# The first x load of a batched matmul issued in two parts, rows 0 to 111 and rows 112 to 127

## The chip, the cores and the metric

The kernel runs on one core of a Trainium2 chip. The metric is the device time of one execution in microseconds (us), taken as the median of several runs. One further execution was recorded by the hardware profiler, and it is the one whose profile is read here.

## The reference

```
b1, b2, m, k, n = 8, 16, 256, 512, 384
x:      (8, 16, 256, 512) float32
weight: (8, 16, 512, 384) float32
out = np.matmul(x, weight).astype(np.float32)     # 128 separate products
```

There are 128 products of a 256x512 matrix with a 512x384 matrix. The inputs are 167.77 MB and the output is 50.33 MB, so that every byte is read or written once.

## The kernel before

**Groups.** The 128 products are worked off in NG = 32 groups of G = 4. A group needs one x load of 2048 KB (`load_x`, L121), weights of 3072 KB (`load_w`, L138), and one store of 1536 KB (`store`, L160). An x load fills one of two buffers `x_sb`, each of 128 partitions (called rows here) with R = 8 rows of x, 16 KB, side by side in each. The first four and the last two groups are "short": their weights come as two loads of 1536 KB, each with a semaphore of its own (`h_in`), the others as one (`w_in`).

**Engines.** VectorE (DVE) turns x into bf16 (`cast_x`, L194, four instructions a group) and casts most of the weights (`cast_w`, L207, and `cast_short`, L223). TensorE (PE) transposes x against an identity (L247) and multiplies (L265; L283 in the last group). ScalarE (ACT) copies the transposed x out of PSUM (L234), casts the rest of the weights (L207) and copies the results out (L300). GpSimd (POOL) makes the identity, and it stores one whole group (SHARED = 26) itself, in three pieces of 5, 120 and 3 rows (`store_rest`, L174).

**The order of the transfers.** SyncE (SP) issues all the other transfers, in an order that is written out by hand in `on_sync`: for each of the first four groups the x load and then the weights, then in a hardware loop x load, store and weights for each group, and at the end the last loads and the last five stores. An issue waits on its engine's own queue: an x load from the third on waits until the cast of the group two before is done (L114), the weights until the casts of the group two before are done (L132, L133). What SP has issued lies in one DMA queue (q1), which 16 DMA engines work off. At its end SP waits for the stores of the three groups before the last (`o_end`, L331), counts a spare semaphore up in a loop of four and PAD = 12 more times (L332 to L335), and waits for the last store (`o_fin`, L336).

**Around the change.** `load_x(e, 0, NG, 0)` is SP's first transfer (L317). `cast_x` waits for it before its first instruction (L190): the semaphore `x_in[0]` must have reached 16, which is what one transfer adds when it has landed. `next_x(0, NG, -1)` (L356) is the first thing that DVE does, and PE's first transposes (L371) and ACT's first copies (L405) follow it.

Of the kernel before, what the change touches and what calls it, by code (L numbers as in the profile page):

```python
# [12 lines left out]
def kernel(  # L13
# [47 lines left out]

    SHARED = NG - 2 - LAG

    ctx.enter_context(tc.tile_critical(sync_engine=mybir.EngineType.Pool, no_gpsimd_drain=True))  # L64

    def sbuf(name, shape, dtype, n):
# [9 lines left out]
    def sems(name, n):  # L76
        return [tc.alloc_semaphore(f"{name}{s}") for s in range(n)]
# [24 lines left out]
    h_in = sems("h_in", G)  # L102
    o_end = sems("o_end", 1)[0]
    rest_out = sems("rest_out", 1)[0]
    o_fin, spare = sems("o_fin", 1)[0], sems("spare", 1)[0]


# [3 lines left out]
    def load_x(e, t, U, s):  # L111
        n = t * U + s
        if not isinstance(n, int) or n >= XS:
            e.wait_ge(x_cast, n * T + (1 - XS) * T)  # L114
        rows = x_rows[bass.ds(n * (G * M), G * M)]
        if is_full(n):
            src = rows.rearrange("(i p r) k -> p i r k", i=G, p=P)
            dst = x_sb[s % XS][:].rearrange("p (i r) k -> p i r k", i=G)
        else:
            src, dst = rows.rearrange("(p r) k -> p r k", r=R), x_sb[s % XS][:]  # L120
        e.dma_start(dst, src).then_inc(x_in[s % XS], 16)  # L121

    def is_short(n):
        return isinstance(n, int) and (n < LAG or n >= NG - 2)

    def is_full(n):
        return isinstance(n, int) and n == NG - 1
# [59 lines left out]
    def cast_x(e, t, U, s, q):  # L187
        n = t * U + s
        if q == 0:
            e.wait_ge(x_in[s % XS], (t * (U // XS) + s // XS) * 16 + 16)  # L190
        e.wait_ge(t_made, n * T + (q + 1 - T + BIAS))  # L191
        rows = slice(2 * q, 2 * q + 2)
        S = SH if is_short(n) else SL
        e.tensor_copy(  # L194
            out=x_bf[s % BS][:, rows].rearrange("p r (s q c) -> p r s q c", s=S, c=KO),
            in_=x_sb[s % XS][:, rows].rearrange("p r (q s c) -> p r s q c", s=S, c=KO),
        ).then_inc(x_cast, 1)
# [116 lines left out]
    def on_sync(e):  # L314
        U = 2
        for n in range(LAG):
            load_x(e, 0, NG, n)  # L317
            load_w(e, 0, NG, n)
        rounds = (NG - 2 - LAG) // U
        with e.Fori(0, rounds) as t:  # L320
            for s in range(U):
                load_x(e, t, U, LAG + s)
                store(e, t, U, s)
                load_w(e, t, U, LAG + s)

        for n in range(LAG + rounds * U, NG):
            load_x(e, 0, NG, n)
            load_w(e, 0, NG, n)
        for n in range(NG - 1 - LAG, NG):
            store(e, 0, NG, n)  # L330
        e.wait_ge(o_end, 16 * (OS - 1))  # L331
        with e.Fori(0, 4):  # L332
            e.sem_inc(spare, 1)
        for _ in range(PAD):
            e.sem_inc(spare, 1)  # L335
        e.wait_ge(o_fin, 16)  # L336

    def on_vector(e):
        U = 2

        def next_x(t, U, s):
            for q in range(T):
                cast_x(e, t, U, s + 1, q)

        def step(t, U, s):
            n = t * U + s
            if is_short(n):
                cast_short(e, n)
            else:
                cast_w(e, t, U, s, range(XV))  # L350
            if not isinstance(n, int) or n < NG - 1:
                next_x(t, U, s)
            if not is_short(n):
                cast_w(e, t, U, s, range(XV, CV), False)

        next_x(0, NG, -1)  # L356
        for n in range(LAG):
            step(0, NG, n)
        rounds = (NG - 3 - LAG) // U
        with e.Fori(0, rounds) as t:  # L360
            for s in range(U):
                step(t, U, LAG + s)
        for n in range(LAG + rounds * U, NG):
            step(0, NG, n)
# [88 lines left out]
```

## Time and profile before

| what | us |
|---|---|
| median of 3 runs | 515.75 (515.63 to 515.79) |
| the profiled execution's own time | 516.01 |
| its span, first to last instruction | 514.2 |
| outside the span | 1.81 |
| DVE busy | 397.6 (77%) |
| ACT busy | 409.5 (80%) |
| PE busy | 316.8 (62%) |
| bytes moved | 218.18 MB, 424 GB/s over the span |

Busy times are sums over an engine's instructions. "DMA share" in a table of windows is the mean busy share of the core's 16 DMA engines in that stretch, as the profile sums it from packets; it can exceed 1.00 by a per cent where packets overlap. "KB" in the lists of transfers is 1024 bytes. "SPq" stands for what SP's queue issues, and "us to landing" is from the issue until the transfer's semaphore has its full count.

### The profile page before, as it was taken

How to read it: one execution, taken by the hardware profiler on the slowest of the kernel's cores; microseconds unless marked ns; L12 is line 12 of the kernel's file. 1: busy time of each engine (PE TensorE's matmuls, PEld its weight loads, DVE VectorE, ACT ScalarE, POOL GpSimd, SP SyncE). 2: the span in 40 equal slices, each digit the busy share in tenths (PEclk: the TensorE clock that was granted, in tenths of full speed). 3: DMA queues.
4: the chain of work that ended last, by engine and by line, in shares of the span. 5: the costliest groups of instructions: out<-in, count | busy, mean ns of one | idle time of the engine just before them, and what ended most of it. 6: DMA issues, size and time to landing. Idle time of an engine off the chain costs nothing.

```text
span 514.2 us, 11664 instructions
## 1 busy us (share of the span) xinstructions
PE 316.8 (62%) x4512; PEld 222.5 (43%) x4512; DVE 397.6 (77%) x462; ACT 409.5 (80%) x387; POOL 3.7 (1%) x9
## 2 busy tenths in 40 slices
PE   2277837556675575866568656567545676474782
PEld 2255525434454343544435534345434354353551
DVE  2788757798777887778977779777798777887980
ACT  1365576997898989789978989987998798989752
POOL 0000000000000000000000000000000000010000
PEclk9687785877787778668776868886878787778887
DMA  8999999999999999999999999999999999999997
GB/s 334 429 427 422 438 423 427 436 430 435 420 427 433 433 436 429 425 429 433 440 427 428 427 435 429 438 426 426 431 437 435 425 426 429 435 435 420 422 426 308
DMA packets 15686, 218.18 MB, mean 424 GB/s; under 512 B 1728, under 2 KB 1728, under 8 KB 3008
## 3 DMA queue, kind: packets, MB, share of 16 engines
q1 hardware_dynamic: 15312, 216.54, 98.8%
q0 software_dynamic: 368, 1.57, 0.7%
q8 instruction: 3, 0.05, 0.0%
q14 instruction: 3, 0.02, 0.0%
HBM read 167.77 MB, written 50.33 MB: 424 GB/s over the span
## 4 chain that ended last, share of the span: by engine, by line
DMA 55%; DVE 31%; issue 9%; PE 1%; DVEq 1%; SPq 1%; ACT 0%; POOLq 0%
DMA w_sb<-in_weight_dram 55%; DVE w_bf L207 20%; DVE w_bf L223 5%; DVE x_bf L194 5%; PE po L283 1%; SPq L138 0%; DVEq L360 0%; SPq L121 0%; DVEq L64 0%; DVEq L203 0%; ACT out_sb L300 0%; SPq L133 0%; DVEq L191 0%; DVEq L217 0%; SPq L448 0%
## 5 line engine op out<-in xcount | busy, mean ns | idle before, releaser
L207 DVE CAST w_bf<-w_sb 32x1536 bf16<-32x1536 f32 x286 | 271.9, 951 | 81.9 <-DMA w_sb<-in_weight_dram 70.7
L265 PE MATMUL po<-w_bf,x_t 128*32 128x384 bf16 x3968 | 197.1, 358 | 34.1 <-DVE w_bf L207 29.5
L247 PE MATMUL pt<-identity,x_bf 128*128 128x128 f32 x512 | 114.7, 414 | 153.5 <-DVE x_bf L194 153.5
L207 ACT CAST w_bf<-w_sb 32x1536 bf16<-32x1536 f32 x130 | 190.9, 1468 | 5.5 <-DMA w_sb<-in_weight_dram 2.3
L247 PEld LDWEIGHTS pt<-identity,x_bf 128*128 128x128 f32 x512 | 103.4, 224 | 165.4 <-issue 165.1
L265 PEld LDWEIGHTS po<-w_bf,x_t 128*32 128x32 bf16 x3968 | 116.1, 105 | 113.8 <-issue 53.0
L300 ACT COPY out_sb<-po 128x768 f32 (+1 forms) x128 | 102.5, 801 | 58.8 <-PE po L265 54.7
L234 ACT COPY x_t<-pt 128x1024 bf16<-128x1024 bf16 x128 | 123.6, 1020 | 21.2 <-PE pt L247 20.6
L194 DVE CAST x_bf<-x_sb 128x1024 bf16<-128x1024 f32 x128 | 79.9, 688 | 12.3 <-DMA x_sb<-in_x_dram 11.5
L223 DVE CAST w_bf<-w_sb 64x1536 bf16<-64x1536 f32 x48 | 45.8, 955 | 7.4 <-DMA w_sb<-in_weight_dram 6.0
L234 ACT ACT_TABLE_LOAD x1 | 1.3, 1283 | 10.6 <-PE pt L247 10.6
L174 POOL DMA_DIRECT2D out_dram<-out_sb x3 | 3.1, 1020 | 458.9 <-DMA out_dram<-out_sb 458.9
L283 PE MATMUL po<-w_bf,x_t 128*128 128x384 bf16 x32 | 5.4, 326 | 0.4 <-DVE w_bf L223 0.4
L283 PEld LDWEIGHTS po<-w_bf,x_t 128*128 128x128 bf16 x32 | 3.1, 98 | 2.7 <-issue 0.7
masks.py:199 POOL TENSOR_SCALAR_AFFINE_SELECT identity<-identity 128x128 f32<-128x128 f32 x1 | 0.3, 283 | 0.2 <-POOL identity L306 0.2
L306 POOL MEMSET identity<- 128x128 f32 x1 | 0.2, 204 | 0.5 <-POOLq L64 0.5
L437 POOL MEMSET const-bfloat16-1.0<- 128x1 bf16 x1 | 0.1, 96 | 0.0
L437 POOL MEMSET const-uint8-127<- 128x1 uint8 x1 | 0.1, 96 | 0.0
L437 POOL MEMSET const-float32-0.0<- 128x1 f32 x1 | 0.1, 93 | 0.3 <-issue 0.3
L437 POOL MEMSET const-float32-1.0<- 128x1 f32 x1 | 0.1, 93 | 0.0
## 6 DMA issues: line engine op xcount, KB each, us to landing
w_sb<-in_weight_dram SPq DMA_DIRECT2D x26, 3072.0 KB, 18.1
x_sb<-in_x_dram SPq DMA_DIRECT2D x32, 2048.0 KB, 22.3
out_dram<-out_sb SPq DMA_DIRECT2D x31, 1536.0 KB, 25.0
w_sb<-in_weight_dram SPq DMA_DIRECT2D x12, 1536.0 KB, 16.7
out_dram<-out_sb POOLq DMA_DIRECT2D x1, 1440.0 KB, 16.8
out_dram<-out_sb POOLq DMA_DIRECT2D x1, 60.0 KB, 7.1
out_dram<-out_sb POOLq DMA_DIRECT2D x1, 36.0 KB, 17.6
```

The source lines that it names most:

```text
L174: e.dma_start(out=dram[p : p + k], in_=out_sb[p : p + k, a : a + R], max_dma_last_dim=R // 2 * N * 4,).then_inc(rest_out, 16)
L194: e.tensor_copy(out=x_bf[s % BS][:, rows].rearrange("p r (s q c) -> p r s q c", s=S, c=KO), in_=x_sb[s % XS][:, rows].rearrange("p r (q s ...
L207: copy(out=w_bf[(s * G + i) % WBS][h * C : (h + 1) * C], in_=w_sb[s % WS][i * C : (i + 1) * C, h * KO : (h + 1) * KO, :],).then_inc(w_vcas ...
L223: e.tensor_copy(out=w_bf[(n * G + d * SH + a) % WBS][h * p : (h + 1) * p], in_=w_sb[n % WS][a * p : (a + 1) * p, r : r + KO, :],).then_inc ...
L234: e.copy(out=x_t[s % TS][:, 2 * q : 2 * q + 2], in_=pt[(s * T + q) % PT][:].bitcast(bf16),).then_inc(t_copied, 1)
L247: ins = e.transpose(pt[(s * T + q) % PT][:, rr, h, :], words[:, 2 * q + rr, h :: KO // 2], identity[:],)
L265: ins = e.matmul(po[(s * T + q) % PO][mine, rr, :N], x_t[s % TS][:, 2 * q + rr, ko // 2, mine, ko % 2], w_bf[(s * G + i) % WBS][:, ko, :], ...
L283: ins = e.matmul(po[(s * T + q) % PO][:, rr, :N], x_t[s % TS][:, 2 * q + rr, ko // 2, :, ko % 2], w_bf[(s * G + q) % WBS][:, ko, :], start ...
L300: e.copy(out=out_sb[:, bass.ds(slot(t, U, s) * R + 2 * q, 2), :], in_=po[(s * T + q) % PO][:, :, :N],).then_inc(o_copied, 1)
L306: e.memset(identity[:], 0.0).then_inc(id_done, 1)
L437: nc = _bacc.Bacc("TRN2", target_bir_lowering=False, num_devices=1)
```

## The change

The first x load, that of group 0, is issued as two transfers. The first has rows 0 to 111 of the buffer (112 x 16 KB = 1792 KB) and counts on a new semaphore `x_rest`; the second has rows 112 to 127 (16 x 16 KB = 256 KB) and counts on `x_in[0]`, as the whole load did. DVE's first cast waits for both. The other 31 x loads and every other instruction stay as they were.

```diff
@@ constants
+    FIRST = 112
@@ semaphores
+    x_rest = sems("x_rest", 1)[0]
@@ load_x
             src, dst = rows.rearrange("(p r) k -> p r k", r=R), x_sb[s % XS][:]
+        if isinstance(n, int) and n == 0:
+            e.dma_start(dst[:FIRST], src[:FIRST]).then_inc(x_rest, 16)
+            dst, src = dst[FIRST:], src[FIRST:]
         e.dma_start(dst, src).then_inc(x_in[s % XS], 16)
@@ cast_x
         if q == 0:
             e.wait_ge(x_in[s % XS], (t * (U // XS) + s // XS) * 16 + 16)
+            if isinstance(n, int) and n == 0:
+                e.wait_ge(x_rest, 16)
         e.wait_ge(t_made, n * T + (q + 1 - T + BIAS))
```

Built, SP's program has one transfer more (112x4096 and 16x4096 elements where 128x4096 stood), and DVE's has no row more: the first cast lists the semaphore x_rest beside the two for which it waited already. PE, ACT and POOL issue the same rows as before.

## The prediction

> **What bounds the kernel now.** I began with the page: its span, the DMA row of the 40 slices, and the chain that ended last.
>
> ```profile
> span 514.2 us, 11664 instructions
> ...
> DMA  8999999999999999999999999999999999999997
> ...
> DMA 55%; DVE 31%; issue 9%; PE 1%; DVEq 1%; SPq 1%; ACT 0%; POOLq 0%
> ```
>
> The DMA engines are nine tenths busy or more in every slice but the first and the last. The chain names DMA for 55%, and DVE for 31%, but DVE's steps on it are those that allow a later load to be issued, and the question is whether the DMA engines ever ran dry while they waited for that. The table of windows answers it.
>
> ```profile
> core 0: us, PE busy (x) PEld busy (x) DVE busy (x) ACT busy (x) POOL busy (x), PEclk, DMA share, GB/s
> 0.00:1.90 1.90, 0.00 (x0) 0.00 (x0) 0.00 (x0) 0.00 (x0) 0.69 (x6) 1.00 0.00 0
> 1.90:4.00 2.10, 0.00 (x0) 0.00 (x0) 0.00 (x0) 0.00 (x0) 0.00 (x0) 1.00 0.96 242
> 4.00:8.00 4.00, 0.00 (x0) 0.00 (x0) 0.00 (x0) 0.00 (x0) 0.00 (x0) 1.00 1.00 428
> 8.00:28.00 20.00, 8.48 (x72) 7.63 (x76) 14.66 (x19) 7.94 (x9) 0.00 (x0) 0.74 1.01 428
> 28.00:508.00 480.00, 308.34 (x4448) 214.90 (x4436) 382.94 (x444) 401.61 (x379) 3.05 (x3) 0.78 1.01 429
> 508.00:510.00 2.00, 0.00 (x0) 0.00 (x0) 0.00 (x0) 0.00 (x0) 0.00 (x0) 0.50 1.00 399
> 510.00:511.00 1.00, 0.00 (x0) 0.00 (x0) 0.00 (x0) 0.00 (x0) 0.00 (x0) 0.50 0.75 298
> 511.00:512.00 1.00, 0.00 (x0) 0.00 (x0) 0.00 (x0) 0.00 (x0) 0.00 (x0) 0.50 0.27 108
> 512.00:513.00 1.00, 0.00 (x0) 0.00 (x0) 0.00 (x0) 0.00 (x0) 0.00 (x0) 0.50 0.09 33
> 513.00:514.20 1.20, 0.00 (x0) 0.00 (x0) 0.00 (x0) 0.00 (x0) 0.00 (x0) 0.50 0.00 0
> ```
>
> The last two columns carry the argument. From about 1.9 us to 510 us the share is full and the rate stands at 428 to 429 GB/s: all 16 engines always have something queued. The kernel is one unbroken DMA stream, with 1.9 us before it and a ragged end. Between 510 and 513 us the share falls over 0.75, 0.27 and 0.09: some engines are done at 510, the last only after 512. So time that a DMA engine loses anywhere, the first load included, is not caught up; it reaches the end if that engine is among the late ones. Time that SP, DVE, ACT or PE lose costs nothing while the queue stays filled.
>
> **The issue itself.** The timeline of SP's queue shows the start.
>
> ```profile
> 0.90 0.39 SPq L121 DMA_DIRECT2D x_sb<-in_x_dram  x1
> 1.35 0.89 SPq L138 DMA_DIRECT2D w_sb<-in_weight_dram  x2
> 2.28 0.64 SPq L121 DMA_DIRECT2D x_sb<-in_x_dram  x1
> 2.97 0.99 SPq L138 DMA_DIRECT2D w_sb<-in_weight_dram  x2
> ...
> 11.18 0.33 SPq L121 DMA_DIRECT2D x_sb<-in_x_dram  x1
> 21.16 0.81 SPq L138 DMA_DIRECT2D w_sb<-in_weight_dram  x2
> ```
>
> One issue takes 0.39 to 0.64 us here. The change adds one, so five issues (two weight loads, the second x load, two more weight loads) come about 0.45 us later. Cover: the first part alone is 112 x 16 KB = 1,835,008 bytes, which at 428 GB/s is 4.29 us of stream from 1.9 us on, and the second part is issued by about 1.8 us, the first weights by about 2.2 us. Without cover it would be 0.45 us; with it, I take 0. The start of the stream should not move: it hangs on the first issue, which stays first. From the trace alone a shorter first issue could start it 0.05 us sooner (an eighth of 0.39).
>
> **The extra wait on DVE.** It comes with the first cast; behind it on DVE stand the whole casting program, behind that PE's first transposes, and SP's third x load.
>
> ```profile
> PE pt L247 <- DVE x_bf L194: 22.7, 3, 10.1
> ...
> DVE x_bf L194 <- DMA x_sb<-in_x_dram: 10.3, 3, 8.7
> ...
> 8.65 2.50 DVE L194 CAST x_bf<-x_sb 128x1024 bf16<-128x1024 f32 x4 [8.65 <-DMA x_sb<-in_x_dram]
> ...
> L121 SPq DMA_DIRECT2D x_sb<-in_x_dram x4: 328/358/642, 0.9 to 24.7; - x4
> ...
> DMA to landing us min/median/max: 7.7/20.9/23.2
> ```
>
> DVE waits 8.7 us for that load already, the first PE and ACT work follows it, and both parts must land as the one load had to: a wait for two costs nothing of its own. If the second part lands L us later, DVE, PE and ACT start L later, and SP's issues at 11.18 and 21.16 us come L later. What covers them is the queue: when the first load lands (0.90 + 7.7 = 8.6 us) there remain four weight loads of 1536 KB and one x load of 2048 KB, 8.39 MB, 19.6 us at 428 GB/s, until about 28 us; with the x load of 11.18 us it reaches 33 us. The weights issued at 21.16 us have some 11 us in hand, so L would have to be over 10 us to open a hole.
>
> **The transfers.** This is the term that decides. The load is 2,097,152 bytes, at 428 GB/s 4.90 us; the second part is an eighth, 262,144 bytes, 0.61 us at the full rate. Does a part of 16 rows run at the full rate? All of SP's transfers in this trace have 128 rows. The nearest rows are GpSimd's three stores, of 5, 120 and 3 rows, which the list of transfers shows with their KB and the median us to landing:
>
> ```profile
> x_sb<-in_x_dram SPq DMA_DIRECT2D x32, 2048.0 KB, 22.3
> out_dram<-out_sb SPq DMA_DIRECT2D x31, 1536.0 KB, 25.0
> w_sb<-in_weight_dram SPq DMA_DIRECT2D x12, 1536.0 KB, 16.7
> out_dram<-out_sb POOLq DMA_DIRECT2D x1, 1440.0 KB, 16.8
> out_dram<-out_sb POOLq DMA_DIRECT2D x1, 60.0 KB, 7.1
> out_dram<-out_sb POOLq DMA_DIRECT2D x1, 36.0 KB, 17.6
> ```
>
> The 120-row store lands no later than a store of 128 rows, so a part with nearly all rows pays nothing that shows. The 5-row store has a 24th of the 120-row store's bytes and takes 7.1 us against 16.8: a narrow transfer is dear for its bytes. How much of the 7.1 is waiting in a full queue the row doesn't tell, so I bound the second part by the rate: at the full rate it costs nothing extra; if rows rather than engines set the pace, 16 rows get an eighth of 428 GB/s, 53.5, and take 4.90 us, which is 4.29 more. (The same bound on the first part, 112 rows at seven eighths, is 0.61 more; by the 120-row store I take 0.) A gain is not excluded by these rows; it would have to come from the ragged end, below. Sixteen rows are nearer to 5 than to 120, which speaks against zero, and the 5-row price is mostly queue, which speaks against the upper end: I take the middle, rounded down, 2.0 us. The weights queue behind the second part on every engine, and the stream has no hole in which to make 2.0 us good.
>
> [...] The rows here show only that 128 rows go at 428 GB/s; none shows a load to 16. [...]
>
> **Sum.** Issue 0, wait 0, first part 0, second part +2.0, end as ragged as before 0. The profiled execution took 516.01 us (514.2 of span and 1.81 around it), so it would take 518.0; it lay 0.26 over the median of 515.75, so the median would be 517.75.
>
> **Rivals.** *The split is free.* If 16 rows are spread over the 16 engines, one row each, at the rate that every row had before, each engine has its eight rows of 16 KB as before and nothing is lost. For it: the same bytes, a full queue behind. Time: 515.75, between -0.05 and +0.5, so 515.7 to 516.25; I put it at 515.8. Chance 0.24.
>
> *The split levels the end.* Faster. If the parts give the engines unequal numbers of rows, and the engines that end late get fewer, the end moves in. In the windows from 510 us the shares add up to 0.75 + 0.27 + 0.09 = 1.11 us, so engines that all ended together would end at 511.1, against somewhat under 513: at most some 1.9 us. A row is 0.61 us of an engine's time (16 x 16,384 bytes at 428 GB/s), so it would take two to three rows less on the late engines; the others would have one more. It decides from 0.6 us on: one row moved off every late engine. Against it: nothing in the trace says that the late engines are the ones that would be spared, and if they aren't, the same 0.61 us a row is added to the end. Time: 515.75 - 1.5 = 514.25. Chance 0.08.
>
> *Both parts go at the pace of their rows.* 4.29 + 0.61 = 4.9 us, 520.65. Against it: the 120-row store shows no such pace. Chance 0.08.
>
> **How the numbers follow.** About 0.2% (1.03 us) is what a measurement of this kernel can tell from no change. My forecast, +2.0, has 0.60, with its own range of +0.9 to +3.25 (516.65 to 519.0), from a part that half overlaps its neighbours to three quarters of the upper bound. Of its 0.60, 0.04 lies within 0.2%. Slower: 0.56 + 0.08 = 0.64. Same: 0.24 + 0.04 = 0.28. Faster: 0.08. The range must take in the free split, and leaves out the 0.08 at either end: 515.5 to 519.0.
>
> **What would show it.** Right: the first cast of DVE starts later than 8.65 us, by about 2 us, at 10 to 11 us; the GB/s of the window 4 to 8 us or the one behind it fall well under 428; from 28 us on the rate is 429 again and every issue of SP is later by the same 2 us; and the last store lands as much later. The free split: the first cast within 0.3 us of its old start, GB/s unchanged. A levelled end: shares in the last 3 us that fall more steeply, with an earlier end. Wrong in its reasoning I would be if the first windows were slower and the end were not, since then the stream had slack that I don't see; or if the DMA share fell under 1.00 between 12 and 508 us, since then SP's later issues had opened a hole.

## The result and the profile after

The changed kernel takes 519.34 us (median of 6 runs, 518.66 to 519.66), the kernel before 515.73 us (515.54 to 516.18). The ratio is 1.0068, with a 95% interval of 1.0057 to 1.0079: slower by 3.6 us. The forecast was 517.75, with a range that ended at 519.0. The profiled execution took 519.25 us, with a span of 517.5 against 514.2.

The table of windows of the changed kernel, in the columns as before:

```profile
1.90:4.00 2.10, 0.00 (x0) 0.00 (x0) 0.00 (x0) 0.00 (x0) 0.00 (x0) 1.00 0.99 296
4.00:8.00 4.00, 0.00 (x0) 0.00 (x0) 0.00 (x0) 0.00 (x0) 0.00 (x0) 1.00 1.02 283
8.00:12.00 4.00, 0.00 (x0) 0.00 (x0) 0.00 (x0) 0.00 (x0) 0.00 (x0) 1.00 0.98 215
12.00:28.00 16.00, 5.57 (x25) 5.20 (x26) 12.64 (x16) 5.73 (x6) 0.00 (x0) 0.79 1.00 421
28.00:508.00 480.00, 318.08 (x4488) 218.74 (x4487) 384.85 (x446) 403.09 (x381) 3.14 (x3) 0.77 1.01 430
508.00:510.00 2.00, 0.41 (x3) 0.02 (x1) 0.00 (x0) 0.80 (x1) 0.00 (x0) 1.00 0.81 344
510.00:511.00 1.00, 0.00 (x0) 0.00 (x0) 0.00 (x0) 0.00 (x0) 0.00 (x0) 1.00 0.88 363
511.00:512.00 1.00, 0.00 (x0) 0.00 (x0) 0.00 (x0) 0.00 (x0) 0.00 (x0) 1.00 0.98 390
512.00:513.00 1.00, 0.00 (x0) 0.00 (x0) 0.00 (x0) 0.00 (x0) 0.00 (x0) 0.95 1.04 412
513.00:514.00 1.00, 0.00 (x0) 0.00 (x0) 0.00 (x0) 0.00 (x0) 0.00 (x0) 0.50 1.01 402
514.00:515.00 1.00, 0.00 (x0) 0.00 (x0) 0.00 (x0) 0.00 (x0) 0.00 (x0) 0.50 0.41 160
515.00:516.00 1.00, 0.00 (x0) 0.00 (x0) 0.00 (x0) 0.00 (x0) 0.00 (x0) 0.50 0.07 27
516.00:517.50 1.50, 0.00 (x0) 0.00 (x0) 0.00 (x0) 0.00 (x0) 0.00 (x0) 0.50 0.00 0
```

The line of the kernel before for 8 to 12 us, which the prediction's table has within 8 to 28:

```profile
8.00:12.00 4.00, 2.55 (x12) 2.58 (x13) 2.50 (x4) 1.36 (x2) 0.00 (x0) 1.00 1.00 427
```

Nearly all of the loss is in two lines: 283 GB/s from 4 to 8 us and 215 from 8 to 12, where the kernel before had 428 and 427. From 28 us on the rate is 430, where it was 429. In bytes: (428 - 283) x 4 + (428 - 215) x 4 + (428 - 421) x 16, less (296 - 242) x 2.1 that the first window gained, makes 1.43 MB, which at 428 GB/s are 3.3 us; the span is 3.3 us longer. Over 480 us a rate that is rounded to 1 GB/s could hide about 1 us, so I also summed the trace's packets: the changed kernel is behind by 3.1 us of bytes at 12 us, 3.3 at 28 us and 3.1 at 505 us. So little was caught up, and nothing more was lost on the way. The end is as ragged as it was, only later: full at 513, and somebody still at work after 515.

The DMA share is 0.98 to 1.02 in every one of these lines from 1.9 to 508 us. The engines counted as busy and moved half to two thirds of the bytes, so this column alone would have shown nothing. Behind 508 us the share falls to 0.81 and 0.88 before it is full once more. The kernel before has such a dip too (0.92 from 506 to 508 us), around the issue of its last store, so its stream was not quite as unbroken to 510 us as the prediction's table, which has 28 to 508 us in one line, made it look.

The timeline (start, duration) and the list of transfers issued in the first 40 us (KB, us to landing):

```profile
0.90 0.40 SPq L125 DMA_DIRECT2D x_sb<-in_x_dram  x1
...
1.37 0.41 SPq L127 DMA_DIRECT2D x_sb<-in_x_dram  x1
...
1.83 1.28 SPq L144 DMA_DIRECT2D w_sb<-in_weight_dram  x2
3.15 0.51 SPq L127 DMA_DIRECT2D x_sb<-in_x_dram  x1
...
12.98 2.50 DVE L202 CAST x_bf<-x_sb 128x1024 bf16<-128x1024 f32 x4 [12.98 <-DMA x_sb<-in_x_dram]
...
15.51 0.33 SPq L127 DMA_DIRECT2D x_sb<-in_x_dram  x1
...
24.41 0.80 SPq L144 DMA_DIRECT2D w_sb<-in_weight_dram  x2
```

```profile
x_sb<-in_x_dram SPq DMA_DIRECT2D x1, 1792.0 KB, 10.9
x_sb<-in_x_dram SPq DMA_DIRECT2D x1, 256.0 KB, 11.6
```

The stream starts where it did, since the first issue is still at 0.90 us. The first part lands 10.9 us after its issue, at 11.8 us, and the second at 1.37 + 11.6 = 13.0 us. The whole load had landed at 8.6 us. DVE's first cast moves from 8.65 to 12.98 us, SP's third x load from 11.18 to 15.51 us, and the weights from 21.16 to 24.41 us.

### The profile page after: what moved, and what is told of

It is laid out like the page before. It is cut to its first block, busy times and chain, and to the rows that moved or that the text cites. A ratio compares the mean times of both kernels' runs of the same rounds, so it can differ in the third digit from the quotient of the medians.

```text
span 517.5 us, 11665 instructions
## 1 busy us (share of the span) xinstructions
PE 324.1 (63%) x4512; PEld 224.0 (43%) x4512; DVE 397.5 (77%) x462; ACT 409.6 (79%) x387; POOL 3.8 (1%) x9
## 4 chain that ended last, share of the span: by engine, by line
DMA 56%; DVE 31%; issue 9%; PE 1%; SPq 1%; DVEq 1%; ACT 0%; POOLq 0%
DMA w_sb<-in_weight_dram 56%; DVE w_bf L215 20%; DVE x_bf L202 5%; DVE w_bf L231 5%; PE po L291 1%; SPq L144 0%; DVEq L368 0%; DVEq L66 0%; SPq L127 0%; DVEq L211 0%; ACT out_sb L308 0%; SPq L139 0%; DVEq L199 0%; SPq L125 0%; DVEq L225 0%
## 5 line engine op out<-in xcount | busy, mean ns | idle before, releaser
L273 PE MATMUL po<-w_bf,x_t 128*32 128x384 bf16 x3968 | 204.3, 368 | 33.7 <-DVE w_bf L215 27.9
L255 PEld LDWEIGHTS pt<-identity,x_bf 128*128 128x128 f32 x512 | 102.3, 224 | 161.4 <-issue 161.0
L273 PEld LDWEIGHTS po<-w_bf,x_t 128*32 128x32 bf16 x3968 | 118.5, 108 | 118.8 <-issue 57.7
## 6 DMA issues: line engine op xcount, KB each, us to landing
x_sb<-in_x_dram SPq DMA_DIRECT2D x1, 1792.0 KB, 10.9
x_sb<-in_x_dram SPq DMA_DIRECT2D x1, 256.0 KB, 11.6
```

Source lines behind the costliest of these rows:

```text
L255: ins = e.transpose(pt[(s * T + q) % PT][:, rr, h, :], words[:, 2 * q + rr, h :: KO // 2], identity[:],)
L273: ins = e.matmul(po[(s * T + q) % PO][mine, rr, :N], x_t[s % TS][:, 2 * q + rr, ko // 2, mine, ko % 2], w_bf[(s * G + i) % WBS][:, ko, :], ...
```

## The experiments

In all of them the kernel before ran on the same chip beside the new one; its medians were 515.62 to 515.77 us. Costs in us are differences of medians. The ratios leave out the new kernel's profiled execution, so the two differ a little where a kernel's times scatter.

**Cut across the rows (e1_cols).** The same two transfers and two semaphores, but every part has all 128 rows.

```diff
-            e.dma_start(dst[:FIRST], src[:FIRST]).then_inc(x_rest, 16)
-            dst, src = dst[FIRST:], src[FIRST:]
+            e.dma_start(dst[:, : R - 1], src[:, : R - 1]).then_inc(x_rest, 16)
+            dst, src = dst[:, R - 1 :], src[:, R - 1 :]
```

> The first x load is still two transfers with two semaphores, but cut across the rows: each part has all 128 rows, the first seven eighths of every row (14 KB), the second the last eighth (2 KB). Theory 'shared paths' (few or unevenly spread rows crowd on a few of the ways into the buffer, and the DMA engines wait for each other): no crowding, 515.75, within 0.5 us of before, first cast at 8.6 to 8.9 us. Rival 'the split itself' (a second transfer, its issue and its semaphore cost the 3.6 us): 519.3, first cast near 13 us.

Measured: 515.76 against 515.77, ratio 1.0001 (0.9992 to 1.0010). The list of its transfers has the same sizes as the changed kernel's:

```profile
x_sb<-in_x_dram SPq DMA_DIRECT2D x1, 1792.0 KB, 7.2
...
x_sb<-in_x_dram SPq DMA_DIRECT2D x1, 256.0 KB, 7.4
```

7.2 us instead of 10.9, for the same 1792 KB issued at the same moment, and 7.4 instead of 11.6; the first cast starts at 8.76 us. The second transfer, its issue and its semaphore cost nothing. What costs is which rows a part has.

**At row 64 (e2_64).**

```diff
-    FIRST = 112
+    FIRST = 64
```

> The same split by rows, but at row 64: rows 0 to 63 and then 64 to 127. [...] 'Only a narrow part is dear' (16 rows cost, 64 hardly): under 517. 'The split itself': 519.3 as with 112.

Measured: 520.50, ratio 1.0091 (1.0075 to 1.0106), 4.7 us more. Its windows:

```profile
4.00:8.00 4.00, 0.00 (x0) 0.00 (x0) 0.00 (x0) 0.00 (x0) 0.00 (x0) 1.00 0.97 205
8.00:12.00 4.00, 0.00 (x0) 0.00 (x0) 0.00 (x0) 0.00 (x0) 0.00 (x0) 1.00 0.99 204
```

205 and 204 GB/s, half of the 428 and 427 of the kernel before, and the first cast starts at 13.46 us where that had 8.65. Two broad parts cost more than a broad and a narrow one (4.7 us against 3.6), so it is not the smallness of a part that is dear.

**The same bytes to other rows (e3_16rows, e4_16step8, e9_32step4).** Eight extra loads of 96 KB each, issued behind the second group's weights into the still unused output buffer; ACT's first copy into that buffer waits for them. Only the rows differ: 16 neighbours, every eighth row (also 16, with 6 KB to a row in both), every fourth row (32, with 3 KB to a row).

```diff
             load_w(e, 0, NG, n)
+            if n == 1:
+                for j in range(8):
+                    dst = out_sb[112:128, 4 * j : 4 * (j + 1), :]     # e3
+                    # e4: out_sb[0:128:8, 4 * j : ...]; e9: out_sb[0:128:4, 2 * j : ...]
+                    ...
+                    e.dma_start(dst, src).then_inc(more, 16)
```

> The kernel before with eight extra loads queued behind the second group's weights, each 6 KB of weights to each of rows 112 to 127 of the output buffer before it is first used (786,432 bytes more in all). At the full 428 GB/s 1.84 us: 517.6. [...] 'Rows set the pace' (16 of 128 rows, an eighth of the rate): 14.7 us, 530.4. 'The split itself', 3.6 us for each extra transfer: 544.

> The same eight extra loads with the same bytes and 16 rows each, but every eighth row (0, 8, ... 120) in place of 16 neighbours. [...] 'Rows set the pace': as with 16 neighbours, 530.4. 'The split itself': as with 16 neighbours.

> [...]

Measured: 524.45, 520.82 and 517.55 us, which is 8.7, 5.1 and 1.9 us over the kernel before (ratios 1.0163, 1.0092 and 1.0036, intervals 1.0147 to 1.0178, 1.0077 to 1.0107 and 1.0022 to 1.0050). The windows in which the extra loads run, of the three kernels in this order:

```profile
28.00:36.00 8.00, 2.38 (x56) 1.22 (x48) 2.18 (x3) 0.00 (x0) 0.00 (x0) 0.94 1.08 106
```

```profile
28.00:32.00 4.00, 1.23 (x32) 0.56 (x24) 1.78 (x2) 0.00 (x0) 0.00 (x0) 1.00 1.05 197
```

```profile
28.00:30.00 2.00, 2.00 (x52) 1.09 (x44) 1.92 (x3) 0.00 (x0) 0.00 (x0) 1.00 1.08 432
30.00:32.00 2.00, 0.07 (x4) 0.00 (x0) 1.94 (x3) 0.39 (x1) 0.00 (x0) 1.00 1.09 464
```

106, 197 and 432 to 464 GB/s, so of 428 a quarter, nearly half, and all. (A window counts a packet whole, its bytes and its time, where it starts. A short window can so read over 428 GB/s, and where slow packets start, a share can lie well over 1.00, as the 1.40 of e10 below.) All three read the same bytes of the weights, and only the rows that they write differ, so the loss hangs on the rows. Their count doesn't explain it: the first two both have 16 and cost 8.7 and 5.1 us, and if it set the price, the 32 rows of e9 would halve that, to 4.3 or 2.5 us; e9 cost 1.9, and its 786,432 bytes take 1.84 at 428 GB/s. What counts is which rows they are. 'Shared paths' would give such an order, but it stays my guess, since no view shows on which way a row is written. The price of the first two is 1.3 and 1.1 us more than their bytes take at 106 and 197 GB/s (7.4 and 4.0 us); where that goes I haven't shown, and the times of e3 (523.74 to 525.90) and of e4 (520.02 to 521.50) scatter as much.

**112 rows and 128 rows (e5_112rows, e6_128rows).** Four extra loads at the same place, 12 KB to a row.

```diff
+                for j in range(4):
+                    dst = out_sb[0:112, 8 * j : 8 * (j + 1), :]     # e6: out_sb[0:128, ...]
+                    ...
```

> The kernel before with four extra loads behind the second group's weights, each 12 KB of weights to each of rows 0 to 111 of the output buffer before it is first used (5,505,024 bytes more). At the full 428 GB/s 12.9 us: 528.6. 'Rows set the pace' (seven eighths of the rate): 14.7 us, 530.4. [...]

> The same four extra loads with all 128 rows (6,291,456 bytes more), the control for 112 rows: all theories 14.7 us at 428 GB/s, 530.4. If it is more, the place of the extra loads costs something by itself, and the price of 112 rows is to be taken against this run.

Measured: 537.49 (ratio 1.0439, 1.0408 to 1.0470) and 530.53 (1.0288, 1.0270 to 1.0307). With 128 rows the four loads cost 14.9 us, as their bytes ask. With 112 rows they move an eighth less and cost 21.8 (the runs lie between 535.96 and 539.97), which is 7.1 us over the 14.7 of 'rows set the pace'. The windows from 32 to 44 us, of e5 and then of e6:

```profile
32.00:44.00 12.00, 0.00 (x0) 0.00 (x0) 2.81 (x3) 0.00 (x0) 0.00 (x0) 0.62 1.00 276
```

```profile
32.00:44.00 12.00, 0.00 (x0) 0.00 (x0) 1.75 (x2) 0.00 (x0) 0.00 (x0) 0.66 1.02 431
```

276 against 431 GB/s: the loads that lacked a single block of 16 rows ran at two thirds of the rate, and the seven eighths that "rows set the pace" would allow (375) are far off. The packets of the two traces say that all rows were slow and not a few: from 32 to 44 us a packet of 12 KB took 0.46 to 0.48 us in e6, and 0.54 to 0.85 in e5. What made them slow isn't shown: no run has 112 rows that aren't neighbours.

**The two parts one by one at the head of the stream (e10_one16, e11_one112).** One extra load into the output buffer: 16 rows right behind the first x load, or 112 rows ahead of it.

```diff
             load_x(e, 0, NG, n)
+            if n == 0:
+                dst = out_sb[112:128]...     # 16 KB a row; e11: out_sb[0:112], ahead of load_x
+                e.dma_start(dst, src).then_inc(more, 16)
```

> The kernel before with one extra load, 16 KB to each of rows 112 to 127 of the output buffer before it is first used, right behind the first x load: the second part's bytes and place, without the first part's crowding. By the rate of the eight such loads (98 to 113 GB/s) 262,144 bytes take 2.5 us, of which 0.61 would be their time at the full rate: 518.2. At the full rate 516.3.

> The kernel before with one extra load, 16 KB to each of rows 0 to 111 of the output buffer, as SP's very first transfer: the first part's bytes and place, without the second part. By the 280 GB/s of the four such loads 1,835,008 bytes take 6.55 us, of which 4.29 at the full rate: 522.2. If the start of the stream gives some of it back (the change lost 3.6 where 2.3 + 1.9 = 4.2 were lost by rate): about 521.6. If a first part of 112 rows costs nothing, as the prediction took it: 519.9.

Measured: 518.29 (ratio 1.0050, 1.0033 to 1.0067) and 522.55 (1.0133, 1.0116 to 1.0150), so 2.7 and 6.9 us. At the full rate their bytes would take 0.6 and 4.3 us. The second part of the change costs about 2.1 us, the first about 2.6. The windows of e10, whose profiled execution took 519.15, and of e11 show each at its place:

```profile
6.00:8.00 2.00, 0.00 (x0) 0.00 (x0) 0.00 (x0) 0.00 (x0) 0.00 (x0) 1.00 1.40 434
8.00:10.00 2.00, 0.00 (x0) 0.00 (x0) 0.00 (x0) 0.00 (x0) 0.00 (x0) 1.00 0.81 94
10.00:12.00 2.00, 0.21 (x1) 0.24 (x2) 1.00 (x2) 0.00 (x0) 0.00 (x0) 1.00 0.78 227
```

```profile
4.00:6.00 2.00, 0.00 (x0) 0.00 (x0) 0.00 (x0) 0.00 (x0) 0.00 (x0) 1.00 1.01 254
6.00:8.00 2.00, 0.00 (x0) 0.00 (x0) 0.00 (x0) 0.00 (x0) 0.00 (x0) 1.00 0.96 303
8.00:10.00 2.00, 0.00 (x0) 0.00 (x0) 0.00 (x0) 0.00 (x0) 0.00 (x0) 1.00 1.00 229
10.00:12.00 2.00, 0.00 (x0) 0.00 (x0) 0.00 (x0) 0.00 (x0) 0.00 (x0) 1.00 0.96 377
```

Together the two would make 4.7 us, and the change lost 3.6. In it the parts overlap: the second lands 1.2 us behind the first (11.8 and 13.0 us), although alone it takes some 2.7 us. The 16 counts by which each semaphore rises show it too: the trace has those of the first part between 8.93 and 11.78 us and those of the second between 10.56 and 12.96. That this overlap makes up the missing 1.1 us is my explanation; no run isolates it.

**Four groups (e7_four).** The change on the x loads of groups 0 to 3.

```diff
-        if isinstance(n, int) and n == 0:
-            e.dma_start(dst[:FIRST], src[:FIRST]).then_inc(x_rest, 16)
+        if isinstance(n, int) and n < LAG:
+            e.dma_start(dst[:FIRST], src[:FIRST]).then_inc(x_rest[n], 16)
```

> The change made to the x loads of the first four groups instead of the first alone, each with a semaphore of its own. 'Shared paths' (the loss is in the stream and adds up wherever the load stands): 4 x 3.6 = 14.4, 530.1. Rival 'the start' (the loss is that DVE, PE and ACT start 4.3 us later, and later loads have slack): 519.3, no more than for the first load.

Measured: 537.01 (534.45 to 538.89; ratio 1.0426, 1.0386 to 1.0466), 21.4 us more. So the loss isn't one of a late start of DVE, PE and ACT, it comes again with each such load. It is larger for the later three, some 5.9 us each against 3.6 for the first. The windows around the later three loads:

```profile
20.00:28.00 8.00, 0.00 (x0) 0.00 (x0) 4.30 (x5) 0.08 (x1) 0.00 (x0) 1.00 1.00 231
36.00:44.00 8.00, 4.60 (x112) 2.60 (x100) 5.49 (x6) 4.02 (x5) 0.00 (x0) 1.00 1.01 231
56.00:64.00 8.00, 1.77 (x40) 0.86 (x32) 3.82 (x4) 1.76 (x3) 0.00 (x0) 0.92 0.98 226
```

The share stays at 0.98 to 1.01 in them, so the queue did not run dry; the slow stretches, 226 to 231 GB/s over 8 us, are simply longer than the first load's. The prices of e5 and e3, also taken in mid-stream, brought to 16 KB a row make 3.0 and 2.3 us over the full rate; as an estimate that is 5.3 for the two parts, close to the 5.9. Why a load in mid-stream loses more than one at its head is open.

**Even and odd rows (e8_evenodd).** Two parts of 64 rows, both spread over all 128.

```diff
+            e.dma_start(dst[0:128:2], src[0:128:2]).then_inc(x_rest, 16)
+            dst, src = dst[1:128:2], src[1:128:2]
```

> The first load in two parts of 64 rows, the even rows and then the odd ones. [...]

Measured: 516.10 against 515.66, ratio 1.0008 (0.9999 to 1.0018), which can't be told from no change; at the row 64 the same two sizes cost 4.7 us. From 4 to 8 us the rate is 409 GB/s here and was 205 there, so the price isn't in the number of rows of a part.

```profile
4.00:8.00 4.00, 0.00 (x0) 0.00 (x0) 0.00 (x0) 0.00 (x0) 0.00 (x0) 1.00 0.96 409
8.00:12.00 4.00, 2.25 (x11) 2.28 (x12) 2.50 (x4) 1.06 (x1) 0.00 (x0) 1.00 1.00 427
```

## Why the prediction was wrong

**What bounds the kernel, the issue and the wait: right.** The stream starts at the same time. The weights' first issue came 0.48 us later (1.83 for 1.35) and the second x load 0.87 us (3.15 for 2.28); the cover held, and e1 with the same issues lost nothing. SP's next two issues came 4.3 and 3.3 us late without opening a hole: the window from 28 to 508 us has 430 GB/s. The loss in the first 28 us, 3.3 us by bytes, came out at the end in full.

**The second part: right in size, by luck.** +2.0 was forecast; alone it costs 2.1 (e10). But the 2.0 was the middle between two bounds, nothing and 4.29 us, and neither holds. That rows and not engines set the pace was only half right: by it 16 rows get an eighth of the rate, 53.5 GB/s, and they had 106 or 197, by which rows they were (e3, e4). At the 106 GB/s of e3 the second part's 262,144 bytes take 2.5 us, as an estimate, which is 1.9 more than at 428.

**The first part: the step that failed.** It was taken at 0, "by the 120-row store", with 0.61 us as its bound. It costs 2.6 us alone (e11), more than the second part, and the four such loads of e5 ran at 276 GB/s. The row that I leaned on couldn't carry this. 16.8 us is GpSimd's time from issue to landing in a full queue, and what that holds of waiting I had noted for the 5-row store and then overlooked for the 120-row one. A landing time in a full queue gives no rate: the x loads of 2048 KB took 22.3 us to land in the median, and at 428 GB/s such a load is 4.9 us of the stream. The bound was too low for the same reason: it supposed that a missing eighth of the rows can cost an eighth of the rate at most, and it cost a third.

**The sum.** 2.0 + 0 should have been 2.1 + 2.6, less 1.1 that I put down to the overlap of the parts: 3.6. The rival in which both parts pay, at 4.9 us with a chance of 0.08, was nearer in its structure, but its mechanism, the pace of the rows, fell with e3, e4 and e9. Free split and levelled end did not occur for this split, nor did the free one for two halves at row 64 (4.7 us, e2); it did for e1 and e8.

**The marks.** "About 2 us later" for the first cast was 4.3 us, and the end was later by 3.3 us of span, not by the same amount. The cast waits for the last of 16 counts, while the end follows the bytes that all engines together were behind (3.1 to 3.3 us of them). The 16 counts of x_in[0] came at 8.01 to 8.63 us before, for the whole load, and at 10.56 to 12.96 in the changed kernel, for the second part, which is 4.3 us later for the last, and 3.1 on average. Why a load of 112 neighbouring rows gets just 276 to 283 GB/s stays open: which engine carries which row isn't in the trace.

## What to carry to other kernels

In this kernel, whose DMA stream hardly pauses (429 GB/s from 28 to 508 us), a load that was split by neighbouring rows slowed the whole kernel (by 3.6 us at row 112 and 4.7 at row 64), although it was issued in time and waited for by nobody new; in one like it, split a load along the row (e1, ratio 1.0001), or into even and odd rows (e8, 1.0008), both of which cost nothing that could be told here. Read the GB/s of a window and not its DMA share, which stood at 0.97 and 0.99 in e2 while the rate was halved (205 and 204 GB/s). A price for a transfer of an unusual shape can't be taken from a time to landing in a full queue (16.8 us for the 120-row store told nothing of the 276 GB/s of e5); it takes the rate of a window in which that shape runs alone, or a run that adds a few such transfers.

## What the runs showed of the hardware that I had not expected

A load of 112 of 128 rows, 12 KB to a row, went at 276 GB/s where 128 rows had 431 (e5, e6), so leaving out 16 rows made a load of fewer bytes slower, 21.8 against 14.9 us for four. And two parts of 64 rows were free as even and odd rows (ratio 1.0008) and cost 4.7 us when split at row 64, with 205 GB/s from 4 to 8 us against 409.
